# A hybrid decoder trunk: where the last head's row sums and its gate product stand in the program

## The chip, the cores and the metric

The kernel runs on one core of a Trainium2 chip. The metric is the device time of one execution in microseconds (us). Before and after are each run several times, and their medians are compared. Next to the runs stands one execution that the hardware profiler recorded; every row of a profile quoted here is from such an execution.

## The reference, cut to what matters

Two layers over 528 tokens (16 meta tokens and 512 of the sequence), model width 1024. Each layer normalises the residual stream, projects it with one large matrix, runs two token mixers side by side, gates their outputs, and adds the merged result back:

```python
h = rmsnorm(h_res, norm_gain[l])
proj = h @ w_in[l]          # u_pool z_pool c_q c_kv k_rope z_mla g_pool g_mla
y_pool = (pool_mix(u_pool, ...) * jax.nn.silu(z_pool)) @ pool_w_up[l]
o_mla = mla(c_q, c_kv, k_rope, pos, ...)            # 8 heads, causal softmax
y_mla = (o_mla * jax.nn.silu(z_mla)) @ mla_w_up[l]
merged = jax.nn.sigmoid(g_pool) * y_pool + jax.nn.sigmoid(g_mla) * y_mla
h_res = h_res + merged @ w_out[l]
```

For the change only the softmax of `mla` counts. A head's output is `exp(s - max) @ v`, divided by the row sum of the exponentials. The kernel leaves the division out of the head and multiplies the gate `silu(z_mla)` by the reciprocals of the row sums instead. The head's values, summed, are multiplied by that gate afterwards.

## The kernel before, in words

**Matrix products.** Every weight tile of 128x512 is fetched from DRAM into one of three buffers called `raw` (`wload`, L193; the fetch is L136, on SyncE's queue, SP), split by ScalarE (L206, `whi`) and VectorE (L207, `wlo`) into a high and a low part, and used by three matmuls for each product (`mm3`, L210: lines 211, 212, 213). A buffer `raw` comes free when L207 has read it; the third next fetch waits for that. Every second tile of `mu` in layer 1 (the second projection after attention, weights `wmu`) goes to a wider pair called `th`.

**The stream.** All products form one list in a fixed order (`register`): in each layer eight tiles `gm0` to `gm7` (the gate of attention, weights `win`), then eight `mu` (`wmu`), then eight `o` (`wout`). A `gm` result is taken out of its PSUM bank by VectorE in L1058; there are four such banks, `mm`. `stream` hands out this list in steps of six matmuls, and `step` (L271) adds each step's nominal time to a counter: 1280 ns with 512 columns (layer 1), 660 ns with 264 (layer 0). A `gm` tile is four steps in layer 1, eight in layer 0. `after(ns, fn)` (L281) registers a piece of other work that is written into the program at the first step at which the counter has gone on by `ns`; this is how attention is woven into the products. `newest[0]` is the last matmul written so far.

**The order on the engines.** The kernel is written in this order, and a planner (`schedule_with_timeline_sim=True`, L1303) then decides the order on each engine: it places an instruction when its inputs are ready by its own model, the one written first ahead of the others. An engine's queue is then fixed and works strictly in that order: on SP an instruction that waits holds all that are behind it. `behind(ins, other)` (L316) makes `ins` wait for `other`; `follow(ins, other)` (L312) sets only the order of two instructions of the same engine, without a wait.

**A head** (`head`, L825). The scores of one head are computed, exponentiated by ScalarE, which also gives the row sums `rs`, and turned in 32x32 blocks by VectorE (L856) into `attD`. The sum of the third part is added in L909, and L910 takes the reciprocals of all row sums. Then, for the head `h`:

- L916 writes the turned blocks to DRAM (`pdr<-attD`, 640 KB). For an odd head `meta_turn` also writes a small block (`mdr<-cq`, L959, written 2600 ns later) and reads it back much later (`racc<-mdr`, L955, three DMAs, 13000 ns later).
- `back` (L921), registered for 7800 ns later, for the last head 2600 ns later, reads the blocks back in an order that finishes the transpose: four DMAs `attE<-pdr` (L924), each behind `newest[0]`, and directly after them, by `follow`, the row sums leave for DRAM: `rdr<-rs`, L927, 2 KB, one piece of 16 bytes from each of 128 partitions.
- `sums` (L930), 2600 ns after `back`, reads the row sums back, spread over 64 partitions: `cq<-rdr`, L934, 128 KB. It needs the row sums to have landed in DRAM.
- `gate` (L936), for odd heads, is the product on GpSimd (L938): gate times reciprocals. For the last head it is registered 7800 ns after the head.
- `parts` (L962) splits the blocks read back (ScalarE L972 `th<-attE`, VectorE L973), and `pv` (L976) multiplies them with the values (TensorE L994 and L997, then L1002 and L1003 take the result out). `part2` (L1007), 6000 ns after the last head's `pv`, adds the meta tokens (TensorE L1009, which reads `racc`; VectorE L1012), multiplies by the gate (L1013) and splits the result for `mu`.

After head 7 the program goes on with gm tiles while head 6 and head 7 are finished (`go`, L1162).

Of the kernel before, what the change touches and what calls it, by code (L numbers as in the profile page):

```python
# [27 lines left out]
H = 8  # L28
# [27 lines left out]
LAG = 2000.0  # L56
TAIL = (9000.0, 9000.0)
SPL = 240
BACK = 7800.0
LATE = 13000.0  # L60
# [21 lines left out]
def trunk(ctx, tc, xT, xrow, mrow, pos, win, wkr, wqb, wkb, wvb, wgr, wpu, wmu, wout, gains, const, yT):  # L82
    nc = tc.nc
    pe, act, dve, gp, sp = nc.tensor, nc.scalar, nc.vector, nc.gpsimd, nc.sync
# [11 lines left out]
    def nm(s):  # L96
        uid[0] += 1
        return f"{s}_{uid[0]}"
# [7 lines left out]
    def att(tag):  # L106
        return sl.tile([P, NB * P], F32 if tag == "D" else F32R, tag=f"att{tag}", name=nm(f"att{tag}"), bufs=1 if tag == "D" else 2)
# [108 lines left out]
    newest = [None]  # L216
# [64 lines left out]
    def after(ns, fn):  # L281
        pend.append((clk[0] + ns, fn))
        pend.sort(key=lambda e: e[0])
# [28 lines left out]
    def follow(ins, other):  # L312
        tc.add_manual_dep(ins.ins, other.ins.name,
                          mybir.DependencyInfo(mybir.DependencyClass.NoSync, mybir.DependencyReason.SCHED_ONLY))

    def behind(ins, other):  # L316
        tc.add_manual_dep(ins.ins, other.ins.name,
                          mybir.DependencyInfo(mybir.DependencyClass.Sync, mybir.DependencyReason.DATA))
# [35 lines left out]
    class Layer:  # L354
# [470 lines left out]
        def head(self, h, kq, prev):  # L825
# [5 lines left out]
            rs = sm.tile([P, 5], F32, tag="rs", name=nm("rs"), bufs=2)  # L831
# [80 lines left out]
            row = rdr[self.l][h]  # L912
# [8 lines left out]
            def back():  # L921
                got.append(att("E"))
                for b in range(4):
                    read = sp.dma_start(got[0][32 * b:32 * b + 32, :].bitcast(F32).rearrange("k (a x) -> k a x", a=4),  # L924
                                        via[:, n * b:n * b + n].rearrange("(a k) x -> k a x", a=4))
                    behind(read, newest[0])
                follow(sp.dma_start(row.rearrange("a (p i) -> p (a i)", i=4), rs[:, 0:4]), read)  # L927
                after(BACK / 3, sums)

            def sums():  # L930
                if odd == 0:
# [4 lines left out]
            def gate():  # L936
                z, rb = self.zms[h // 2][:, NM:T].rearrange("p (i q) -> p i q", i=4), self.rb
                behind(gp.tensor_mul(z, z, rb[:, 0:512].rearrange("p (q i) -> p i q", i=4)), newest[0])  # L938

            after(BACK if h + 1 < H else BACK / 3, back)  # L940
            if odd == 1:
                after(LATE if h + 1 < H else BACK, gate)
            return h, got

        def meta_turn(self, pm):
# [362 lines left out]
```

## Time and profile before

| what | us |
|---|---|
| runs before | 755.31, 755.49, 753.53 |
| their median | 755.31 |
| the profiled execution, its own time | 755.48 |
| its span, first to last instruction | 753.7 |
| TensorE busy in the span | 748.1 |

The span is what the profile shows; 1.78 us of the profiled execution's own time lie around it (755.48 - 753.7). In rows of the timeline the first number is the start in us from the span's start, the second the duration; then come engine, line, operation, and the tiles as out<-in with the count of instructions merged into the row. In brackets stands how long the engine was idle before it, and what ended that. SPq is SP's queue: a row there is the issue of a DMA, not the transfer. In the chain of waits a row is start, duration, engine or DMA, and line or tiles; there the duration of a DMA is the time from its issue to its landing.

### The profile page before, as it was taken

What the parts mean: (1) busy time and instruction counts of PE and PEld (TensorE: products, weight loads), DVE (VectorE), ACT (ScalarE), POOL (GpSimd) and SP (SyncE); (2) the same over time, 40 slices, a digit from 0 to 9 for tenths busy, and PEclk for the clock granted to TensorE, in tenths of its full rate; (3) what the DMA queues carried; (4) which work ended last, traced back from release to release, by engine and by line L of the source; (5) the groups of instructions that cost most, each with busy time, mean ns of one, the idle gap of its engine ahead of it and who ended that gap; (6) DMA issues with size and microseconds to landing.
All of it is one profiled execution on the core that took longest, in us unless ns stands there. A gap on an engine that the chain in (4) does not pass through costs nothing.

```text
span 753.7 us, 14317 instructions
## 1 busy us (share of the span) xinstructions
PE 748.1 (99%) x5010; PEld 681.9 (90%) x5010; DVE 562.3 (75%) x1214; ACT 395.2 (52%) x864; POOL 241.8 (32%) x294
## 2 busy tenths in 40 slices
PE   9999999999999999999999999999999999999998
PEld 9999899999999999999997898887788888887887
DVE  5588777658999987694367478678589999966942
ACT  6755656554656555543254456455445665554321
POOL 2126404704552520161130264038043526102400
PEclk9999999999999999999999999999999999999999
DMA  8633223434766576425643332233356666763462
GB/s 280 179 103 118 70 81 91 112 96 142 206 163 177 170 202 176 129 91 165 183 135 91 108 113 73 82 91 107 105 151 216 181 175 189 203 167 98 129 223 87
DMA packets 72798, 106.55 MB, mean 141 GB/s; under 512 B 14051, under 2 KB 34915, under 8 KB 72726
## 3 DMA queue, kind: packets, MB, share of 16 engines
q1 hardware_dynamic: 72582, 105.38, 47.8%
q8 instruction: 39, 0.64, 0.4%
q14 instruction: 33, 0.27, 0.1%
q10 hardware_dynamic: 144, 0.26, 0.1%
HBM read 89.76 MB, written 15.85 MB: 140 GB/s over the span
## 4 chain that ended last, share of the span: by engine, by line
PE 94%; DMA 4%; SPq 1%; DVE 1%; ACT 0%; issue 0%; ACTq 0%; DVEq 0%
PE mm L211 28%; PE mm L213 28%; PE mm L212 28%; PE S L211 2%; PE S L213 2%; PE S L212 2%; DMA raw<-wmu 1%; PE o L994 1%; DMA rdr<-rs 1%; PE o L997 1%; PE S L891 1%; PE S L538 1%; PE S L504 0%; DMA raw<-win 0%; DMA cq<-rdr 0%; DMA xb<-xT 0%
## 5 line engine op out<-in xcount | busy, mean ns | idle before, releaser
L213 PE MATMUL mm<-hh,wlo 128*128 128x264 f32 (+2 forms) x1072 | 337.0, 316 | 0.0
L212 PE MATMUL mm<-hl,whi 128*128 128x264 f32 (+2 forms) x1072 | 336.4, 315 | 0.0
L211 PE MATMUL mm<-hh,whi 128*128 128x264 f32 (+2 forms) x1072 | 336.3, 315 | 0.0
L207 DVE TENSOR_TENSOR wlo<-raw,whi 128x512 fp32r<-128x512 f32 (+2 forms) x239 | 179.6, 754 | 87.5 <-ACT whi L206 83.9
L206 ACT ACTIVATE whi<-raw 128x512 fp32r<-128x512 f32 (+2 forms) x239 | 143.0, 600 | 167.3 <-PE mm L212 133.2
L211 PEld LDWEIGHTS mm<-hh,whi 128*128 128x128 f32 x1072 | 201.4, 188 | 14.1 <-DVE vt L704 0.8
L212 PEld LDWEIGHTS mm<-hl,whi 128*128 128x128 f32 x1072 | 201.6, 188 | 13.0
L213 PEld LDWEIGHTS mm<-hh,wlo 128*128 128x128 f32 x1072 | 200.9, 188 | 12.3
L652 POOL TENSOR_TENSOR racc<-racc,tmp 128x264 f32<-128x264 f32 (+1 forms) x15 | 14.9, 993 | 117.7 <-ACT tmp L651 117.7
L1069 POOL TENSOR_TENSOR tmp<-tmp,xb 128x264 f32<-128x264 f32 (+1 forms) x24 | 27.7, 1166 | 41.8 <-DVE tmp L1067 39.7
L821 POOL CAST qhl<-q 32x528 fp32r<-32x528 f32 (+1 forms) x32 | 27.6, 876 | 40.5 <-PE S L891 39.1
L843 DVE CUSTOM_DVE_ANT_0 S<-S,maskw,nqs 128x240 f32<-128x240 f32 (+4 forms) x80 | 37.9, 493 | 1.5 <-PE S L213 1.3
L211 PE MATMUL mm<-cq,whi 128*128 128x264 f32 (+1 forms) x108 | 34.7, 321 | 0.0
L212 PE MATMUL mm<-th,whi 128*128 128x264 f32 (+1 forms) x108 | 34.6, 321 | 0.0
L213 PE MATMUL mm<-u,wlo 128*128 128x264 f32 (+1 forms) x108 | 34.5, 320 | 0.0
L212 PE MATMUL mm<-cq,whi 128*128 128x264 f32 (+1 forms) x108 | 34.5, 321 | 0.0
L213 PE MATMUL mm<-cq,wlo 128*128 128x264 f32 (+1 forms) x108 | 34.5, 321 | 0.0
L211 PE MATMUL mm<-u,whi 128*128 128x264 f32 (+1 forms) x108 | 34.5, 319 | 0.0
L938 POOL TENSOR_TENSOR u<-u,cq 128x512 f32<-128x512 f32 x8 | 12.9, 1616 | 64.6 <-DMA cq<-rdr 41.2
L853 POOL COPY pm<-cq 128x16 f32<-128x16 f32 x32 | 17.9, 559 | 44.4 <-ACT cq L850 42.3
L850 ACT ACTIVATE cq<-S,bia 128x400 f32<-128x400 f32 (+2 forms) x48 | 24.4, 512 | 13.9 <-DVE bia L904 12.8
L973 DVE TENSOR_TENSOR attE<-attE,th 128x640 fp32r<-128x640 f32 x32 | 25.6, 828 | 6.1 <-ACT th L972 6.1
(305 smaller groups left out, 1401.2 us busy)
## 6 DMA issues: line engine op xcount, KB each, us to landing
raw<-win SPq DMA_DIRECT2D x143, 256.0 KB, 3.5
pdr<-attD SPq DMA_DIRECT2D x16, 640.0 KB, 3.6
attE<-pdr SPq DMA_DIRECT2D x64, 160.0 KB, 3.6
raw<-wout SPq DMA_DIRECT2D x32, 256.0 KB, 3.0
raw<-wpu SPq DMA_DIRECT2D x16, 256.0 KB, 2.7
raw<-wmu SPq DMA_DIRECT2D x16, 256.0 KB, 2.7
raw<-wqb SPq DMA_DIRECT2D x12, 256.0 KB, 2.6
xb<-xT SPq DMA_DIRECT2D x8, 264.0 KB, 5.6
```

What stands on the lines that cost most here:

```text
L206: act.activation(hi[:, :n], raw[:, :n], AF.Copy)
L207: dve.tensor_sub(lo[:, :n], raw[:, :n], hi[:, :n].bitcast(F32))
L211: first = pe.matmul(out, wh, xh, start=start, stop=False)
L212: pe.matmul(out, wh, xl, start=False, stop=False)
L213: newest[0] = pe.matmul(out, wl, xh, start=False, stop=stop)
L652: self.acc_last = gp.tensor_add(self.acc[:, a:b], self.acc[:, a:b], t[:, :b - a])
L821: gp.tensor_copy(d[r0:r0 + 32, x0:T], f[gq:gq + 32, x0:T])
L843: return dve.tensor_tensor_reduce(out=sv, in0=sv, in1=mask, scale=nqs[:, i, h:h + 1], scalar=3e38, op0=ALU.add, op1=ALU.min, accum_out=bia ...
L850: act.activation(pv, sv, AF.Exp, scale=-1.0, bias=bia[:, i:i + 1], accum_out=rs[:, c:c + 1])
L853: gp.tensor_copy(pm[:, i, 16 * odd:16 * odd + 16], pt[i][:, 0:NM])
L973: dve.tensor_sub(got[:, a:b], f[:, a:b], hi[:, a:b].bitcast(F32))
L1069: gp.tensor_add(t[:, :b - a], t[:, :b - a], self.am[m][:, a:b])
```

## The change

Only head 7 of each layer is touched (`h + 1 < H` is false). For the other heads the row leaves as before.

- The row sums of head 7 (the DMA of L927) are written into the program 2000 ns (`LAG`) of the step counter after `back`, where before they were written together with it. They no longer follow the last of the four reads; they are behind the newest matmul at that point.
- `sums` of head 7 comes 4600 ns after `back` where before it came 2600 ns after it; the distance between row and `sums` stays 2600.
- The gate product of the last head comes 9800 ns after the head where before it came 7800 ns after it.

No DMA, no product and no byte is added or removed.

```diff
-                follow(sp.dma_start(row.rearrange("a (p i) -> p (a i)", i=4), rs[:, 0:4]), read)
-                after(BACK / 3, sums)
+
+                def leave():
+                    follow(sp.dma_start(row.rearrange("a (p i) -> p (a i)", i=4), rs[:, 0:4]), read)
+                    after(BACK / 3, sums)
+
+                if h + 1 < H:
+                    leave()
+                else:
+                    after(LAG, lambda: behind(sp.dma_start(row.rearrange("a (p i) -> p (a i)", i=4), rs[:, 0:4]), newest[0]))
+                    after(LAG + BACK / 3, sums)
...
             if odd == 1:
-                after(LATE if h + 1 < H else BACK, gate)
+                after(LATE if h + 1 < H else BACK + LAG, gate)
```

## The prediction, made before the changed kernel was run

> **What bounds the kernel now.** I read the page first: the share of each engine, then who waited for whom, for TensorE and for SP's queue, then the chain of waits at the two places where head 7 ends.
>
> ```profile
> span 753.7 us, 14317 instructions
> PE 748.1 (99%) x5010; PEld 681.9 (90%) x5010; DVE 562.3 (75%) x1214; ACT 395.2 (52%) x864; POOL 241.8 (32%) x294
> ```
>
> TensorE is busy for 748.1 of 753.7 us. The whole list of what it waited for is three rows:
>
> ```profile
> PE mm L211 <- DVE cq L1058: 1.1, 1, 1.1
> PE wps L158 <- DVE na L774: 1.1, 1, 1.1
> PE S L994 <- ACT th L972: 0.2, 1, 0.2
> ```
>
> The second is the start of the kernel (the warming matmuls of L158), which the change doesn't reach. What any change of attention's order can win is therefore the first and the third row, about 1.3 us, which is under 0.2%. What it can lose has no such bound. The first row, on TensorE's timeline:
>
> ```profile
> 685.93 0.39 PE L212 MATMUL mm<-kn,th 128*128 128x512 f32 x1
> 686.16 0.40 PE L213 MATMUL mm<-q,th 128*128 128x512 f32 x1
> 687.70 0.47 PE L211 MATMUL mm<-q,whi 128*128 128x512 f32 x1 [1.14 <-DVE cq L1058]
> ```
>
> Matmuls of this shape start 0.23 us apart (685.93, 686.16); the next starts 1.54 us later. So the stall is 1.54 - 0.23 = 1.3 us, counted from start to start. The matmul is the first of `mu2` in layer 1 and waits for the bank that `gm7` leaves. The chain of waits says why that bank is late, and shows the same form in layer 0:
>
> ```profile
> 297.94 0.41 SPq L934
> 298.45 3.49 DMA raw<-win
> 302.58 1.36 ACT th L972 x2
> ...
> 669.51 4.02 DMA rdr<-rs
> 673.61 0.45 SPq L934
> 674.15 5.58 DMA raw<-wmu
> ...
> 680.41 0.79 DVE th L207
> 681.22 2.70 DMA raw<-wmu
> ...
> 684.69 0.68 DVE th L207
> 686.86 0.70 DVE cq L1058
> ```
>
> From the top of the lower part: head 7's row sums take 4.02 us to land. `sums` (L934) stands on SP until then, and a weight fetch behind it leaves only at 674.15. Its cast ends at 681.20, so the buffer `raw` comes free late, the next fetch leaves at 681.22, its cast (684.69) holds VectorE's queue, and the bank's L1058 comes last, at 686.86. In layer 0 it is shorter: a `win` fetch leaves behind L934 at 298.45, ScalarE's cast of it stands in front of L972, and L994 waits 0.2 us. Both stalls of TensorE begin at **SP waiting in L934 for the row sums of head 7**.
>
> **Where the row goes.** The title of the change says later. SP's queue in layer 1 and layer 0 says what "later" is measured against:
>
> ```profile
> 664.47 0.32 SPq L916 DMA_DIRECT2D pdr<-attD  x1
> 665.24 0.33 SPq L136 DMA_DIRECT2D raw<-win  x1
> 666.41 0.32 SPq L959 DMA_DIRECT2D mdr<-cq  x1
> 667.72 1.75 SPq L924 DMA_DIRECT2D attE<-pdr  x4
> 669.51 1.75 SPq L927 DMA_DIRECT2D rdr<-rs  x1
> 671.30 0.43 SPq L136 DMA_DIRECT2D raw<-win  x1
> 671.83 0.38 SPq L136 DMA_DIRECT2D raw<-wmu  x1
> ```
>
> ```profile
> 287.30 0.54 SPq L916 DMA_DIRECT2D pdr<-attD  x1
> 291.31 0.32 SPq L924 DMA_DIRECT2D attE<-pdr  x1
> 294.83 0.43 SPq L927 DMA_DIRECT2D rdr<-rs  x1
> 295.30 0.43 SPq L136 DMA_DIRECT2D raw<-win  x1
> 297.90 0.45 SPq L934 DMA_DIRECT2D cq<-rdr  x1
> ```
>
> The reads wait for the blocks to land in DRAM (issue 664.47, first read 667.72), and the row waits behind them because `follow` says so. Its own inputs are earlier. After the change it needs two things: the reciprocals, and the newest matmul one `LAG` after `back`. By the step counter `back` of layer 1 is written when `gm4` is half done and the row when `gm4` is complete; in layer 0 it is when the first of the two segments of `gm3` is complete. VectorE's rows give bounds for both (first layer 1, then layer 0, with the L1058 that takes this result out):
>
> ```profile
> 665.13 0.17 DVE L910 RECIPROCAL rs<-rs 128x4 f32<-128x4 f32 x1
> 666.38 0.69 DVE L1058 TENSOR_TENSOR cq<-mm,rinv 128x512 f32<-128x512 f32 x1
> 671.40 0.68 DVE L207 TENSOR_TENSOR wlo<-raw,whi 128x512 fp32r<-128x512 f32 x1
> ```
>
> ```profile
> 286.54 0.15 DVE L910 RECIPROCAL rs<-rs 128x4 f32<-128x4 f32 x1
> 290.65 0.41 DVE L1058 TENSOR_TENSOR cq<-mm,rinv 128x264 f32<-128x264 f32 x1
> ```
>
> Counting the L1058 of layer 1 back from 686.86 (`gm7`), 666.38 takes out `gm4`; the matmul is done by then. So the row can leave between 665.30 and 666.38, on a queue that is idle from 665.57 to 666.41 and from 666.73 to 667.72: **before the reads, about 3 to 4 us earlier than now**, not later. In layer 0 it can leave between 287.84, when SP is through with the blocks, and 290.65; the reads start at 291.31. The planner does pass instructions over others: the `wmu` fetch at 671.83 is written after `sums`, and leaves before it (673.61).
>
> **The change part by part.**
>
> - The row's DMA is neither added nor made larger, only moved past `mdr` and the four reads. Its issue (0.43 us in layer 0; 1.75 in layer 1) falls in the 2.15 us between 665.57 and 667.72, of which `mdr` takes 0.32. Both fit with 0.1 us left; a delay of the reads is bounded by 1.75 us and taken as 0, since 0.43 is the nearer row (a rival below prices the other end).
> - The added wait for the matmul: it holds SP, where `mdr`, the reads and the fetches are queued. Its end is at most 666.38, before `mdr` leaves now. Below it is 0, above it 666.38 - 665.57 = 0.8 us, still covered by the wait for the blocks until 667.72. Taken as 0.
> - `sums`, written two steps later than now: its matmul is in the first half of `gm5`, which is taken out at 670.80 at the latest (the next L1058 after 666.38 in VectorE's order); what decides is the row's landing:
>
> ```profile
> DMA to landing us min/median/max: 3.3/3.6/4.1
> 670.80 0.67 DVE L1058 TENSOR_TENSOR cq<-mm,rinv 128x512 f32<-128x512 f32 x1
> ```
>
> With the longest of the 16 rows, 665.6 + 4.1 = 669.7. The reads are issued by 669.47. So `sums` follows them almost without a wait, at about 669.7 (670.8 at worst), and the 1.75 us that the row takes now at 669.51 are free for it. The two fetches follow at about 670.2 and 670.7, where they leave at 671.30 and 671.83 now.
>
> - The next fetch, now at 674.15, then waits only for its buffer, which L207 frees at 671.40 + 0.68 = 672.08. It leaves at 672.1, **2.05 us earlier**. If the 1.3 us by which one issue is longer than the others (1.75 against 0.43) falls on another DMA of this stretch, it is still 672.4, 1.75 us earlier. With 5.58 us to landing, as now, the whole lower part of the chain moves forward by 1.75 to 2.05 us, more than the stall of 1.3. Gain: 1.3 us. What is late next is nothing in this stretch: after 687.70 no row of TensorE's waits follows.
> - In layer 0 the fetch at 298.45 waits for L934, which ends at 297.9; without it, it leaves behind the fetch at 295.30, some 2 us earlier. Gain: the 0.2 us of the third row.
> - The gate, 2000 ns later in the program: no DMA, one product on GpSimd, which waits for `sums`, and its reader L1013 comes after `pv` of head 7 and another 6000 ns of steps. Taken as 0; if it were late, GpSimd's next work would be late with it, which is that of `mu`.
>
> Sum: 755.48 - 1.3 - 0.2 = 753.98, so **754.0 us**, against a median of 755.31 that lies 0.17 us below the profiled execution. The forecast is a gain of 1.3 us, or 0.2%. The measurement tells about 0.3% (2.3 us) from no change, so this counts as the same.
>
> A rule that speaks against the change: the Trainium skill, page "DMA: Bandwidth & Descriptors", section "Queues, rings and completion order", has it that each DMA engine takes up the descriptors of a ring in the order of issue. By that rule the row, now ahead of the reads on the same queue, delays their data, which no row of this trace shows. The sum by it is the third rival's.
>
> **The rivals.**
>
> 1. *The wait is moved and not removed* (slower). If the planner puts the row where its words say, behind the reads and the two fetches, the row leaves at about 670.5 (669.47 and two issues of about 0.5). `sums` then holds SP until 670.5 + 4.02 = 674.5, the fetch leaves at 675.0 instead of 674.15, and the stall grows by 0.85: 756.3 us, layer 0's stall left as it is. The point from which it decides: the row's issue plus 4.02 has to be under 672.1 for the full gain, so it must leave before 668.1, ahead of the reads; at 669.51 nothing changes, and each us beyond costs one. With a landing of `racc` that is as much later, L1009 could add up to another us. For it: the words of the change; against it: the inputs are there 3 us before the reads.
> 2. *The transfer, not the queue, is the limit.* The fetch lands 5.58 us after its issue, the next one 2.70. If those 2.9 us are other transfers in its way, an earlier issue brings no earlier landing. Layer 1's stall stays, layer 0's goes: 755.3 us. For it: 5.58 against 2.70; against it: the reads and both earlier fetches would also be issued no later than now.
> 3. *The row delays the reads.* Then L972 of head 7, which waits for them, is late:
>
> ```profile
> 673.37 1.37 ACT L972 ACTIVATE th<-attE 128x640 fp32r<-128x640 f32 x2 [2.70 <-DMA attE<-pdr]
> 675.90 0.40 PE L994 MATMUL S<-th,vt 128*128 128x512 f32 x1
> ```
>
> L972 ends at 674.74, L994 starts at 675.90: 1.16 us of cover. The whole 1.75 us of delay cost 0.6 us: 754.6 us.
>
> 4. *The planner turns something else.* A new order on SP can put a cast on VectorE ahead of a bank's L1058 at another place, as 684.69 stands ahead of 686.86 now. One such stall of 1.3 us without the gains: 756.8 us; two, 758.1.
>
> **How the numbers follow.** The forecast has 0.55, the first rival 0.17, the second 0.12, the third 0.06, the fourth 0.10. The likeliest is 754.0. For the range, the runs before differ by 2 us among themselves (753.53 to 755.49), so I go down to 752.8 and up to 757.0, past the first and the first half of the fourth rival. Faster by over 0.3% (under 753.05) would need more than both stalls, so only the spread of runs: 0.06. Slower by over 0.3% (above 757.6) needs the first rival with a late `racc`, or two new stalls: 0.13. The rest, 0.81, is within 0.3%.
>
> **What would show it.** Right: on SP `rdr<-rs` of head 7 stands between the blocks' write and the first read in both layers; L934 follows the reads within half a us; the fourth next fetch leaves at about 672 and no longer right behind L934; TensorE's list of waits has only the start of the kernel. Wrong: `rdr<-rs` behind a read, L934 more than 2 us behind the DMA before it, or a row of waits for L1058, L972 or L1009 on TensorE. The prediction as a whole is wrong if a stall shows at a place that has nothing to do with head 7.

## The result, and the profile after

The changed kernel takes 755.78 us (median of 21 executions, 754.93 to 759.2), the kernel before, beside it on the same chip, 754.86 us (21 executions, 753.53 to 756.19). The ratio is 1.0017, with a 95% interval of 1.0010 to 1.0025; it is estimated from all executions of both, and isn't the quotient of the two medians (755.78 / 754.86 = 1.0012). The forecast was 754.0 us and a gain of 1.3 us. The time lies within 0.3% and inside the range, but the sign is the other one: a small, measurable loss. The profiled execution took 755.15 us with a span of 753.4, so 1.75 us lie around it, as before (1.78).

The page's first lines for the changed kernel, then the whole list of what TensorE waited for (us in total, times, longest us):

```profile
span 753.4 us, 14319 instructions
PE 748.4 (99%) x5010; PEld 682.3 (91%) x5010; DVE 562.2 (75%) x1214; ACT 395.7 (53%) x864; POOL 239.7 (32%) x294
```

```profile
PE wps L158 <- DVE na L774: 1.1, 1, 1.1
PE S L1002 <- ACT th L980: 0.4, 1, 0.4
PE S L1005 <- DVE attE L981: 0.3, 1, 0.3
```

Behind the changed place the lines stand 8 further down: the split L972 and L973 is now L980 and L981, the matmuls of `pv` L994 and L997 are L1002 and L1005, `sums` L934 is L942, the gate product L938 is L946. Head 7's row leaves in L935, `mdr` in L967, `racc` in L963.

Both stalls that the prediction wanted to remove are gone from the list (L211 behind the bank, and layer 0's). Two others stand in their place, both in `pv` of head 7 in layer 1. SP's queue at that place, to be held against the same stretch of before:

```profile
663.52 0.32 SPq L916 DMA_DIRECT2D pdr<-attD  x1
664.29 0.33 SPq L136 DMA_DIRECT2D raw<-win  x1
664.72 0.72 SPq L935 DMA_DIRECT2D rdr<-rs  x1
665.54 0.40 SPq L967 DMA_DIRECT2D mdr<-cq  x1
666.72 1.75 SPq L924 DMA_DIRECT2D attE<-pdr  x4
669.54 0.45 SPq L942 DMA_DIRECT2D cq<-rdr  x1
670.09 0.53 SPq L136 DMA_DIRECT2D raw<-win  x1
670.67 1.75 SPq L136 DMA_DIRECT2D raw<-wmu  x2
```

The row leaves ahead of `mdr` and the reads, and `sums` behind the reads and ahead of all three fetches. The reads are issued 3.20 us after the blocks (666.72 - 663.52), against 3.25 before (667.72 - 664.47). So their issue isn't late. Layer 0 shows the same order:

```profile
288.32 0.88 SPq L935 DMA_DIRECT2D rdr<-rs  x1
289.29 0.41 SPq L967 DMA_DIRECT2D mdr<-cq  x1
290.75 3.43 SPq L924 DMA_DIRECT2D attE<-pdr  x4
294.27 0.45 SPq L942 DMA_DIRECT2D cq<-rdr  x1
```

What is late is what the reads bring. ScalarE, VectorE and GpSimd of the changed kernel in layer 1, and then the rows of VectorE and GpSimd before:

```profile
674.90 1.37 ACT L980 ACTIVATE th<-attE 128x640 fp32r<-128x640 f32 x2 [4.75 <-DMA attE<-pdr]
675.67 2.04 DVE L981 TENSOR_TENSOR attE<-attE,th 128x640 fp32r<-128x640 f32 x1 [4.45 <-ACT th L980]
675.48 1.55 POOL L946 TENSOR_TENSOR u<-u,cq 128x512 f32<-128x512 f32 x1 [12.37 <-DMA cq<-rdr]
```

```profile
674.15 1.56 DVE L973 TENSOR_TENSOR attE<-attE,th 128x640 fp32r<-128x640 f32 x2 [2.07 <-ACT th L972]
679.08 1.55 POOL L938 TENSOR_TENSOR u<-u,cq 128x512 f32<-128x512 f32 x1 [15.02 <-DMA racc<-mdr]
```

Two things are to be seen. The cast L980 starts 674.90 - 666.72 = 8.18 us after the first read is issued; before it was 673.37 - 667.72 = 5.65. And the first half of VectorE's split takes 2.04 us, where both halves together took 1.56: the gate product on GpSimd, which the program now holds later, starts 3.6 us *earlier* than in this first profile of before (675.48 against 679.08), 0.19 us ahead of the split. (In a second profile of the kernel before, g1_before_again below, it starts at 676.82.) TensorE's timeline shows what the two cost:

```profile
675.50 0.40 PE L213 MATMUL mm<-hh,wlo 128*128 128x512 f32 x1
676.32 0.51 PE L1002 MATMUL S<-th,vt 128*128 128x512 f32 x1 [0.42 <-ACT th L980]
...
677.81 0.40 PE L213 MATMUL mm<-hh,wlo 128*128 128x512 f32 x1
678.50 0.45 PE L1005 MATMUL S<-attE,vt 128*64 128x512 f32 x1 [0.29 <-DVE attE L981]
```

From start to start the steps are 0.82 and 0.69 us, where 0.23 is usual: (0.82 - 0.23) + (0.69 - 0.23) = 0.59 + 0.46 = 1.05 us.

The chain of waits (start, duration, what) had the row sums' landing, SP in L934 and two fetches at this place before. Now it has one fetch, the split and `pv`:

```profile
671.25 6.35 DMA raw<-wmu
677.65 0.80 DVE attE L981
678.50 0.45 PE S L1005
```

The link from the fetch to the split is only inferred, from the fetch having landed last; L981 doesn't read `raw`. The rows of VectorE and GpSimd above say what held it.

### The profile page after: what moved, and what is told of

Same layout as the page of the kernel before. It is cut to its first block, busy times and chain, and to the rows that moved or that the text cites. A ratio compares the mean times of both kernels' runs of the same rounds, so it can differ in the third digit from the quotient of the medians.

```text
span 753.4 us, 14319 instructions
## 1 busy us (share of the span) xinstructions
PE 748.4 (99%) x5010; PEld 682.3 (91%) x5010; DVE 562.2 (75%) x1214; ACT 395.7 (53%) x864; POOL 239.7 (32%) x294
## 4 chain that ended last, share of the span: by engine, by line
PE 98%; DMA 1%; DVE 0%; ACT 0%; issue 0%; DVEq 0%
PE mm L213 29%; PE mm L211 29%; PE mm L212 29%; PE S L211 2%; PE S L213 2%; PE S L212 2%; PE o L1002 1%; PE o L1005 1%; DMA raw<-wmu 1%; PE S L891 1%; PE S L538 1%; PE wps L158 1%; PE S L504 0%; PE mm L1017 0%; PE S L1005 0%; PE mm L710 0%
## 5 line engine op out<-in xcount | busy, mean ns | idle before, releaser
L213 PE MATMUL mm<-hh,wlo 128*128 128x264 f32 (+2 forms) x1072 | 337.0, 316 | 0.0
L211 PE MATMUL mm<-hh,whi 128*128 128x264 f32 (+2 forms) x1072 | 336.2, 315 | 0.0
L207 DVE TENSOR_TENSOR wlo<-raw,whi 128x512 fp32r<-128x512 f32 (+2 forms) x239 | 181.5, 762 | 84.3 <-ACT whi L206 78.5
L211 PEld LDWEIGHTS mm<-hh,whi 128*128 128x128 f32 x1072 | 201.4, 188 | 14.0 <-DVE vt L704 0.8
L213 PEld LDWEIGHTS mm<-hh,wlo 128*128 128x128 f32 x1072 | 200.9, 188 | 12.3
L821 POOL CAST qhl<-q 32x528 fp32r<-32x528 f32 (+1 forms) x32 | 25.7, 818 | 39.5 <-PE S L891 38.2
L211 PE MATMUL mm<-cq,whi 128*128 128x264 f32 (+1 forms) x108 | 34.7, 321 | 0.0
L213 PE MATMUL mm<-u,wlo 128*128 128x264 f32 (+1 forms) x108 | 34.5, 320 | 0.0
L213 PE MATMUL mm<-cq,wlo 128*128 128x264 f32 (+1 forms) x108 | 34.5, 321 | 0.0
L211 PE MATMUL mm<-u,whi 128*128 128x264 f32 (+1 forms) x108 | 34.5, 319 | 0.0
L981 DVE TENSOR_TENSOR attE<-attE,th 128x640 fp32r<-128x640 f32 x32 | 27.2, 877 | 7.7 <-ACT th L980 7.7
L946 POOL TENSOR_TENSOR u<-u,cq 128x512 f32<-128x512 f32 x8 | 13.1, 1643 | 61.0 <-DMA cq<-rdr 56.6
```

What stands on the lines that cost most here:

```text
L207: dve.tensor_sub(lo[:, :n], raw[:, :n], hi[:, :n].bitcast(F32))
L211: first = pe.matmul(out, wh, xh, start=start, stop=False)
L213: newest[0] = pe.matmul(out, wl, xh, start=False, stop=stop)
L821: gp.tensor_copy(d[r0:r0 + 32, x0:T], f[gq:gq + 32, x0:T])
L981: dve.tensor_sub(got[:, a:b], f[:, a:b], hi[:, a:b].bitcast(F32))
```

## The experiments

The theory after the result, called theory A in the expectations: the row's DMA, 128 pieces of 16 bytes, ahead of the reads makes them land late, and `pv` of head 7 in layer 1 waits for the cast. Next to it stands a second claim: the stall of 1.3 us that was to be won is not in every execution. The rivals: the reads wait for their place in SP's queue, or for the read back of `sums`; the fetches behind the earlier read back of `sums` are what is late (theory B in the expectations); the loss is in layer 0 or elsewhere. All numbers of the table are from the profiled executions, in layer 1; "delay" is from the issue of the first read to the start of the cast. Times are medians, with the kernel before on the same chip beside them; the ratio is estimated as above. A kernel that ran once has its one time, which decides nothing on the time.

| kernel | ahead of the reads | delay us | time / before us | ratio, 95% interval |
|---|---|---|---|---|
| before (first profile) | nothing | 5.65 | | |
| g1_before_again | nothing | 6.33 | 753.79 / 755.00, one execution | |
| e1_layer0_only | nothing | 6.34 | 754.19 / 754.15 | 0.9999, 0.9990 to 1.0008 |
| e3_row_held | nothing | 6.23 | 754.17 / 754.15 | 1.0003, 0.9993 to 1.0012 |
| g3_row_behind_fetches | nothing | 6.20 | 754.34 / 755.00 | 0.9994, 0.9986 to 1.0003 |
| after | the row, 128 x 16 B | 8.18 | 755.78 / 754.86 | 1.0017, 1.0010 to 1.0025 |
| e2_layer1_only | the row | 8.74 | 755.82 / 754.15 | 1.0018, 1.0005 to 1.0032 |
| e4_double_row | the row, twice | 7.68 | 755.82 / 754.15 | 1.0019, 1.0011 to 1.0028 |
| f3_row_on_act | the row, ScalarE's queue | 7.56 | 755.39 / 753.92 | 1.0018, 1.0009 to 1.0027 |
| g2_gate_late | the row | 8.99 | 755.43 / 755.00 | 1.0007, 0.9997 to 1.0016 |
| f1_small_ahead | 128 x 16 B, nobody reads | 8.02 | 754.86 / 753.92 | 1.0016, 1.0007 to 1.0026 |
| g4_few_ahead | 16 x 16 B | 7.43 | 755.60 / 755.00, one execution | |
| j2_pieces_32 | 128 x 32 B | 5.67 | 754.31 / 754.33, one execution | |
| h3_pieces_64 | 128 x 64 B | 6.37 | 753.30 / 754.11, one execution | |
| h4_pieces_256 | 128 x 256 B | 6.40 | 754.36 / 754.11, one execution | |
| f2_wide_ahead | 128 x 512 B | 6.51 | 754.37 / 753.92 | 1.0006, 0.9998 to 1.0015 |

The delay is a measure of the landing. The trace keeps 16 landing marks of each read; half of those of the last read are in 4.7 to 5.0 us after the first read's issue where nothing stands ahead, and 6.0 to 6.5 us after it in the six kernels with 128 or more pieces of 16 bytes. In f1_small_ahead and f3_row_on_act the last mark (674.86 and 675.18) stands 0.1 us in front of the cast (674.96 and 675.29); the bracket of these two rows names a matmul that ended at the same time.

**Which layer: e1_layer0_only and e2_layer1_only.** The first has the change in layer 0 alone (the condition gets `or self.l != 0`), the second in layer 1 alone:

```diff
-                if h + 1 < H:
+                if h + 1 < H or self.l != 1:
...
-                after(LATE if h + 1 < H else BACK + LAG, gate)
+                after(LATE if h + 1 < H else BACK + LAG * (self.l == 1), gate)
```

> The change made in layer 0 alone; layer 1 as before. Theory A (the row ahead of the reads makes head 7's blocks land late, and the product with the values waits): in layer 0 the reads land late too (5.7 us instead of 3.0 to 3.3) but the product is far enough behind, so TensorE shows no wait there; the 0.2 us of the kernel before go, layer 1 keeps its own. 0 to 0.3 us faster than before, ratio 0.9995 to 1.0. Theory B (the fetches behind the earlier read of the row sums are what is late): the fetches of gm6 and gm7 in layer 0 land late, a wait of TensorE on a cast there, about 0.5 us slower, ratio 1.0005 to 1.001.

> The change made in layer 1 alone; layer 0 as before. Theory A: all of the loss is here. TensorE waits in L1002 and L1005 of head 7 for L980 and L981, 0.7 us or more together, L980 stands idle over 4 us for the reads; ratio that of the whole change, 1.001 to 1.0025. Theory B: no more than half of the loss, ratio 1.0 to 1.001, with a wait on a cast (L206, L207).

Layer 0 alone changes nothing, layer 1 alone gives the loss of the whole change. TensorE's waits of e2_layer1_only at head 7, and the reads and their cast in e1_layer0_only:

```profile
PE S L1002 <- ACT th L980: 1.0, 1, 1.0
PE S L1005 <- DVE attE L981: 0.3, 1, 0.3
```

```profile
666.57 1.74 SPq L924 DMA_DIRECT2D attE<-pdr  x4
672.91 1.37 ACT L980 ACTIVATE th<-attE 128x640 fp32r<-128x640 f32 x2 [3.12 <-DMA attE<-pdr]
```

In e1_layer0_only layer 1 has the order of before, and the wait at L211 that the first profile showed there is not in its list (which has 0.3 us at another L211, 5 us after the start of the kernel). Its span is 751.8 us. In its layer 0 the row is ahead of the reads too, but nothing waits for them there: by the landing marks the last read is in at 297.27, and ScalarE starts its cast only at 299.84, behind a cast of weights.

**The row kept behind the reads: e3_row_held.** The row is written at the later point of the change and also follows the last read, which gives SP the order of before.

```diff
+                    def leave_late():
+                        ins = sp.dma_start(row.rearrange("a (p i) -> p (a i)", i=4), rs[:, 0:4])
+                        follow(ins, read)
+                        behind(ins, newest[0])
...
+                    after(LAG, leave_late)
```

> The change with one line more: the row is written as late as in the change, and is also kept behind the last read. The row sums, their read and the gate product have the change's places in the program, but on SP the row cannot pass the reads. Theory A: the loss is gone, as is the gain: ratio 1.0 within 0.0008, TensorE's waits are those of before (L1058's bank, up to 1.3 us). Theory B or a cost of the later gate product: the loss stays, ratio 1.001 or more.

The loss is gone, and there is no gain either. The expectation missed in one point: the wait of before, at L211 for the bank, isn't there. TensorE waits for nothing but the start of the kernel:

```profile
PE wps L158 <- DVE na L774: 1.1, 1, 1.1
```

**The kernel before once more: g1_before_again.** No edit.

> The kernel before once more, for a second profile of it. If its stall of 1.3 us before mu2 stands in every execution: TensorE waits about 1.1 us for L1058 again, span 753.5 or more. If it depends on how the transfers fall in one execution: no such wait, span 751.8 to 752.3, as in the two variants whose layer 1 has the order of before.

Its list of TensorE's waits has only the start of the kernel, and its span is 752.0 us, not 753.7. SP's queue, with ScalarE's cast of the reads, shows where it parts from the first profile:

```profile
667.41 1.74 SPq L924 DMA_DIRECT2D attE<-pdr  x4
669.20 0.43 SPq L927 DMA_DIRECT2D rdr<-rs  x1
669.67 0.44 SPq L136 DMA_DIRECT2D raw<-win  x1
...
673.74 1.37 ACT L972 ACTIVATE th<-attE 128x640 fp32r<-128x640 f32 x2 [3.35 <-DMA attE<-pdr]
673.88 0.45 SPq L934 DMA_DIRECT2D cq<-rdr  x1
674.43 0.54 SPq L136 DMA_DIRECT2D raw<-wmu  x1
```

`sums` still waits until 673.88 (673.61 in the first profile), and the fetch behind it leaves at 674.43, even later than 674.15. Yet no stall follows. Two things differ. The row's issue is shorter, 0.43 us against 1.75, and with it the fetch of `win` leaves earlier, 669.67 against 671.30. And the fetch behind `sums` lands sooner: its cast starts 3.7 us behind its issue (678.17 - 674.43), where the first profile shows 5.58 us to landing. The first alone doesn't make the stall: j2_pieces_32 (below) has a row issue of 1.72 us there, its fetch behind `sums` leaves at 674.20, and it has no stall either. Its cast starts 4.4 us behind that issue:

```profile
678.63 0.63 ACT L206 ACTIVATE th<-raw 128x512 fp32r<-128x512 f32 x1 [1.70 <-DMA raw<-wmu]
```

So the order of the queue alone doesn't make the 1.3 us; they came with the late landing of that fetch in one execution. Why it landed late there stays open.

**The row alone, with nothing that depends on it: f1_small_ahead and f2_wide_ahead.** To the kernel before, an extra write to DRAM is added ahead of `mdr` and the reads of layer 1; nobody reads it. In f1 it has the row's shape, 128 pieces of 16 bytes; in f2 it has 128 pieces of 512 bytes, 32 times the bytes.

```diff
+                if self.last and h + 1 == H:
+                    behind(sp.dma_start(spare_row.rearrange("a (p i) -> p (a i)", i=4), cst[:, 0:4]), made)
```

> The kernel before, with one DMA more in layer 1: 128 pieces of 16 bytes of the constants go to a DRAM tensor that nobody reads, at the place on SP where the change puts the row (before mdr and the reads of head 7). Row, sums and gate product stay. If it is the small pieces ahead of the reads that make them late: over 4 us idle in front of L972 of head 7, TensorE waits 0.4 to 1.4 us in L994, ratio 1.001 to 1.003. If the earlier read of the row sums (L934 ahead of the fetches) makes the loss: no wait in L994, ratio 0.9995 to 1.0005.

> The same with 128 pieces of 512 bytes (64 KB) in place of 16 bytes. If any DMA to DRAM ahead holds the reads, or its bytes count: reads as late as with the small pieces or later, ratio 1.001 to 1.003. If only the small pieces do it: the reads are late by no more than the 64 KB take, 0.2 to 0.5 us, within the cover of 1.2 us, no wait in L994, ratio 0.9995 to 1.0005.

SP, ScalarE and the wait of TensorE in f1_small_ahead, then SP and ScalarE in f2_wide_ahead (the split is L976 in both):

```profile
664.90 0.73 SPq L926 DMA_DIRECT2D sprow<-cst  x1
666.94 1.75 SPq L928 DMA_DIRECT2D attE<-pdr  x4
675.09 0.45 SPq L938 DMA_DIRECT2D cq<-rdr  x1
674.96 1.36 ACT L976 ACTIVATE th<-attE 128x640 fp32r<-128x640 f32 x2 [4.93 <-PE mm L212]
```

```profile
PE S L998 <- ACT th L976: 0.6, 1, 0.6
```

```profile
667.78 1.74 SPq L928 DMA_DIRECT2D attE<-pdr  x4
674.29 1.37 ACT L976 ACTIVATE th<-attE 128x640 fp32r<-128x640 f32 x2 [3.54 <-DMA attE<-pdr]
```

The 2 KB write makes the cast 1.7 us later than in g1_before_again (8.02 against 6.33) and brings the wait and the loss. With the 64 KB write it is 0.2 us later, which is within the 0.7 us by which the kernels with nothing ahead differ, and `pv` doesn't wait. f2's time tells less than its trace: its interval reaches from no change to most of the loss. In f1 the read back of `sums` leaves only at 675.09, after the cast has begun: it cannot be what holds the reads. So the first rival (place in the queue) and the second (`sums`) are out; the bytes are not it either.

**How many pieces: e4_double_row and g4_few_ahead.** e4 is the changed kernel with the row written twice, the second time to spare DRAM; g4 is f1 with 16 pieces.

```diff
+                        behind(sp.dma_start(spare_row[self.l].rearrange("a (p i) -> p (a i)", i=4), rs[:, 0:4]), newest[0])
```

```diff
-                    behind(sp.dma_start(spare_row.rearrange("a (p i) -> p (a i)", i=4), cst[:, 0:4]), made)
+                    behind(sp.dma_start(spare_row[:, 0:64].rearrange("a (p i) -> p (a i)", i=4), cst[0:16, 0:4]), made)
```

> The change, with the row of head 7 written twice, the second time to a DRAM tensor that nobody reads (one DMA of 2 KB more in each layer). Theory A with the row's pieces of 16 bytes as what holds the reads: reads land later still by 0.5 to 2 us, the wait in L1002 grows by as much, ratio against before 1.002 to 1.004. If only the issue of one more DMA counts: its 0.4 us lie in SP's idle time before the reads, ratio as the change, 1.001 to 1.0025.

> The variant with the extra small DMA ahead of the reads in layer 1, with 16 pieces of 16 bytes in place of 128, one for each DMA engine. If each piece costs its part (8 for each engine make 1.5 us): the reads are late by 0.2 us, their first packets come as without it, no wait in L994. If one small piece holds an engine as long as eight: reads late by 1.5 us, the median of their packets 3.8 to 4.1 us behind the first issue instead of 2.4, a wait of 0.4 us or more.

Twice the pieces didn't add: 7.68 us of delay against 8.18, ratio 1.0019 against 1.0017 (TensorE's wait was longer, 1.4 us, but e2_layer1_only, with one row, has 1.0). So the expected growth didn't come. An eighth of the pieces still gave 7.43 us and 0.9 us of wait, in one execution. By the other sign that the expectation for g4 named it came out the first way: half of the last read's landing marks are in after 5.1 us, as with nothing or wide pieces ahead (4.7 to 5.2), against 6.5 in f1; only the last mark is late (7.33 us, against 5.6 to 6.2 with nothing ahead). So the delay of the cast is not in proportion to the pieces, but with 16 of them most of the data come as without; that the price doesn't depend on the count is not shown.

**Which queue: f3_row_on_act.** The row is issued from ScalarE's DMA queue.

```diff
-                    after(LAG, lambda: behind(sp.dma_start(row.rearrange("a (p i) -> p (a i)", i=4), rs[:, 0:4]), newest[0]))
+                    after(LAG, lambda: behind(act.dma_start(row.rearrange("a (p i) -> p (a i)", i=4), rs[:, 0:4]), newest[0]))
```

> The change, with head 7's row issued from ScalarE's DMA queue instead of SP's, in both layers. If what counts is the place ahead of the reads on the same queue: the reads land as before (L980 idle for about 3 us), no wait in L1002, and the row still lands early, ratio 0.9985 to 1.0003. If the pieces hold the 16 DMA engines whatever queue they come from: reads late again, ratio 1.001 to 1.0025.

```profile
665.38 0.33 ACTq L935 DMA_DIRECT2D rdr<-rs  x1
667.73 1.74 SPq L924 DMA_DIRECT2D attE<-pdr  x4
675.29 1.36 ACT L980 ACTIVATE th<-attE 128x640 fp32r<-128x640 f32 x2 [4.64 <-PE mm L213]
```

The delay is 7.56 us and the loss remains (1.0018, 1.0009 to 1.0027). The order within one queue's ring, which the prediction took from the Trainium skill as the ground of its third rival, is therefore not needed for it. The Trainium skill, page "DMA: Bandwidth & Descriptors", section "Issuing engines are not separate DMA queues", says that DMAs of all issuing engines run on the same 16 engines and interleave there; this run agrees.

**Which size: j2_pieces_32, h3_pieces_64, h4_pieces_256.** f2 with narrower pieces; the edit is only the width (8, 16 or 64 numbers).

```diff
-                    behind(sp.dma_start(spare, cst[:, 0:128]), made)
+                    behind(sp.dma_start(spare[:, 0:8], cst[:, 0:8]), made)
```

> The kernel before with an extra write of 128 pieces of 32 bytes ahead of the reads of layer 1. Pieces of 16 bytes gave 8.0 us from the first read to the cast, pieces of 64 bytes 6.4. If a limit in size lies at or below 32 bytes: 6.2 to 6.5 us. If it lies above 32: 7.5 to 8.7. In between if the cost falls off evenly from 16 to 64 bytes.

> The kernel before with an extra write of 128 pieces of 64 bytes ahead of the reads of layer 1. If the count of pieces under some size holds the reads, whatever the bytes, the cast of the reads starts 7.5 to 8.7 us after the first read is issued, as with pieces of 16 bytes. If the cost falls off evenly between 16 and 512 bytes, about 7.5 us. If only pieces of 16 bytes do it, 6.2 to 6.5 us.

> The same with 128 pieces of 256 bytes. Under a limit in size that lies at 512 bytes: 7.5 to 8.7 us from the first read to the cast, as with 16 bytes. With a cost that falls off evenly: about 7 us. With a limit below 256 bytes: 6.2 to 6.5 us.

SP and ScalarE of j2_pieces_32, then of h3_pieces_64:

```profile
667.59 1.75 SPq L928 DMA_DIRECT2D attE<-pdr  x4
673.26 1.37 ACT L976 ACTIVATE th<-attE 128x640 fp32r<-128x640 f32 x2 [2.71 <-DMA attE<-pdr]
```

```profile
666.08 1.75 SPq L928 DMA_DIRECT2D attE<-pdr  x4
672.45 1.37 ACT L976 ACTIVATE th<-attE 128x640 fp32r<-128x640 f32 x2 [2.91 <-DMA attE<-pdr]
```

None of the three holds the reads (5.67, 6.37 and 6.40 us, one execution each); the wait of 0.7 us in h4's list is in layer 0. j2 lies below all that was forecast for it, like the first profile of before (5.65), with which it shares the long issue behind the reads. There is no even fall from 16 to 512 bytes: pieces of 16 bytes did it, pieces of 32 didn't. One thing was not kept apart: the pieces of 16 bytes stand next to each other in DRAM, the wider ones lie 512 bytes apart. Whether it is the size or the neighbourhood was not tried.

**The gate product: g2_gate_late.** The changed kernel, in layer 1 with the gate product 8000 ns further on; SP's order stays.

```diff
-                after(LATE if h + 1 < H else BACK + LAG, gate)
+                after(LATE if h + 1 < H else BACK + LAG + 8000 * self.last, gate)
```

> The change, with the gate product of head 7 in layer 1 written 8000 ns later; the order on every engine is that of the change. If the gate product on GpSimd, running beside L981 on VectorE, makes that one long (2.77 us for two instead of 1.56) and so the wait in L1005: L981 takes 1.56 us again, the wait in L1005 (0.3) goes, the wait in L1002 stays; ratio 0.0002 to 0.0005 under that of the change, 1.0005 to 1.002. If the two have nothing to do with each other: L981 2.77 us and the wait as in the change.

```profile
676.84 1.56 DVE L981 TENSOR_TENSOR attE<-attE,th 128x640 fp32r<-128x640 f32 x2 [5.38 <-DMA racc<-mdr]
678.78 1.83 POOL L946 TENSOR_TENSOR u<-u,cq 128x512 f32<-128x512 f32 x1 [15.33 <-PE mm L213]
```

```profile
PE S L1002 <- ACT th L980: 1.5, 1, 1.5
```

The split is back at 1.56 us and the wait at L1005 is gone, while the late cast stays (8.99 us, and 1.5 us of wait). The ratio is 1.0007, 0.9997 to 1.0016; the interval doesn't tell it from no change, and overlaps that of the change. What shows the stretch is the trace, not the time.

**More cover for the late cast: f4_pv_held, h1_cover_more, h2_pv_held_again, j1_held_and_gate_late.** The changed kernel with `pv` of head 7 in layer 1 later: nine matmuls (f4, and again as h2), three matmuls (h1), nine matmuls and the late gate of g2 (j1).

```diff
-            hosts, last = list(hosts), [None]
+            hosts, last = list(hosts), [newest[0] if self.last and h + 1 == H else None]
...
-            fill_now(2600)
+            fill_now(7680 if self.last else 2600)
```

```diff
-            fill_now(2600)
+            fill_now(5200 if self.last else 2600)
```

> The change, with the product of head 7 with its values in layer 1 placed 9 matmuls (2.1 us) later among those of gm7; VectorE and ScalarE take the cast for mu2 before that for mu3. If the loss is only that product's wait for late blocks (up to 1.6 us): it goes, TensorE waits for nothing but the start, ratio 0.9985 to 1.0003. If late fetches or anything else made the loss: ratio stays 1.001 or more, with a wait elsewhere.

> The change, with head 7's pv in layer 1 three matmuls of gm later (0.69 us at 0.23 us each); the orders of ScalarE, VectorE, GpSimd and SP are those of the change. Theory (the reads land late behind the small pieces, and the loss is TensorE's wait for the cast of them): the wait at L1002 falls from 0.4-1.5 to 0-0.8 us, the time lies halfway between the change and the kernel before, ratio 1.0005 to 1.0012. Rival (the loss is something other than that wait, spread over the stage): ratio 1.0015 to 1.0020, as for the change itself.

> The kernel of f4_pv_held once more, nine matmuls of cover (2.1 us). If the wait at L1002 is the whole loss, the executions lie at the kernel before, 0.9995 to 1.0005, with no second group 3 us above. If the order of casts that comes with it costs time of its own, the second group of some 3 us more shows again, and the profile, if it falls on one, has a wait at L211 for VectorE or ScalarE.

> The change with both waits met at once in layer 1: nine matmuls of cover ahead of head 7's pv, and the gate product 8000 ns later, so that it no longer starts ahead of VectorE's half of the split. The row stays ahead of the reads. Theory (the loss is the late cast and the stretched split, nothing else): L981 takes 1.56 us, no wait at L1002 or L1005, ratio 0.9995 to 1.0006. Rival (the stage loses something besides these two waits): ratio 1.0009 or more, as for h2_pv_held_again or the change itself.

| kernel | time / before us | ratio, 95% interval | wait at L1002 | wait at L1005 |
|---|---|---|---|---|
| f4_pv_held | 755.03 / 753.92 | 1.0022, 1.0010 to 1.0034 | none | none |
| h1_cover_more | 755.49 / 754.11 | 1.0022, 1.0013 to 1.0031 | none | 0.8 |
| h2_pv_held_again | 754.75 / 754.11 | 1.0009, 1.0000 to 1.0019 | none | 1.0 |
| j1_held_and_gate_late | 755.61 / 754.33 | 1.0013, 1.0002 to 1.0024 | none | 0.8 |

f4's profiled execution (754.18) is one of its faster ones; that it shows no wait doesn't explain the median of 755.03. Three matmuls of cover took the wait from L1002 and put it at L1005, with the time as before: my expectation for h1 missed, since it reckoned with the late cast alone, and the stretched split is the later of the two. Nine matmuls took some of the loss at most. In j1 the gate product, though later in the program, started 0.1 us ahead of the second half of the split, and that half was stretched to 2.18 us:

```profile
677.03 2.92 DVE L981 TENSOR_TENSOR attE<-attE,th 128x640 fp32r<-128x640 f32 x2 [4.28 <-ACT th L980]
```

```profile
677.67 1.59 POOL L946 TENSOR_TENSOR u<-u,cq 128x512 f32<-128x512 f32 x1 [12.94 <-PE mm L213]
```

So j1 didn't make the state that it was made for (its list also has 0.5 us at L213, in layer 0), and it decides nothing on whether the two waits are the whole loss. f4 had four of its twelve executions at 757.1 to 757.9 us; the same kernel as h2 had none above 755.9 in eleven. These four stay unexplained.

**The words of the change taken literally: g3_row_behind_fetches.** The kernel before with the row of layer 1 really later: behind the reads and two fetches, `sums` behind the third fetch and `racc`, the gate 7500 ns later.

```diff
-                follow(sp.dma_start(row.rearrange("a (p i) -> p (a i)", i=4), rs[:, 0:4]), read)
-                after(BACK / 3, sums)
+                def leave():
+                    ins = sp.dma_start(row.rearrange("a (p i) -> p (a i)", i=4), rs[:, 0:4])
+                    follow(ins, read)
+                    if last:
+                        behind(ins, newest[0])
+                    after(BACK / 3, sums)
...
+                if last:
+                    after(7500, leave)
```

> The kernel before, with head 7's row of layer 1 put where the words of the change put it: behind the reads and also behind the two next weight fetches; its read (L942 or near) comes behind the third fetch and racc. If small pieces hold what comes behind them in the DMA engines: the reads land as before, no wait in L994; the third fetch and racc are the ones held, by about 1.5 us, which the cover may or may not take: ratio 0.9985 to 1.001, at most the stall before mu2 of 1 us. If the row's place makes no difference as long as the reads are ahead of it: ratio 0.9995 to 1.0005.

With nothing ahead of the reads (6.20 us of delay) the time is 0.9994 of before, 0.9986 to 1.0003: not to be told from it. No kernel of this study is clearly faster than the kernel before.

## Why the prediction was wrong, step by step

- **Where the row goes: right.** It stands between the blocks and the first read in both layers, 1.20 us after the issue of the blocks in layer 1 (664.72 - 663.52; the bounds were 0.83 to 1.91). `sums` follows the reads, and all three fetches come behind it. The added wait for the matmul costs nothing, since the reads are issued no later.
- **`sums` without a wait: nearly right.** It starts 1.07 us behind the reads' last issue (669.54 against 666.72 + 1.75), not within half a us: the row took up to 4.82 us from its issue (669.54 - 664.72), more than the 4.1 that was reckoned. The fetch that left at 674.15 now leaves at 671.25, and the old stall is gone; but it takes 6.35 us to land, not the 5.58 that the sum took over.
- **The gain of 1.3 us: mis-sized, in most of the profiled executions there was nothing to win.** The step took a stall from one profiled execution for a property of the queue's order. In g1_before_again, e1_layer0_only and e3_row_held, which have the same order there, `pv` and `mu2` in layer 1 wait for nothing. The sign of it stood in the numbers given: the profiled execution (755.48) was among the slower ones shown, 1.95 us above the fastest (753.53), which is more than the whole stall. In layer 0 the mechanism was right: the cast in front of L994 starts at 300.54 in the changed kernel and at 299.84 in e1_layer0_only, against 302.58 before, and the wait is gone in both. But that wait is 0.2 us in the first profile, 0.7 in h4_pieces_256 and none in g1_before_again, which have the same order there, and it is too small for e1's time to show it (0.9999, 0.9990 to 1.0008).
- **The step that failed: "a delay of the reads is bounded by 1.75 us and taken as 0".** The row is not free ahead of the reads. In the six kernels of the table that have 128 or more pieces of 16 bytes ahead, the cast comes 7.56 to 8.99 us after the first read; where nothing stands ahead, 5.65 to 6.34. (With more cover, in f4, h1, h2 and j1, it is 7.85 to 8.44.) The price is 1.2 to 3.3 us of delay, 1.85 for the changed kernel against g1_before_again (8.18 - 6.33): not 0, and not bounded by 1.75. The bound was wrong because it took the issue's duration for the whole price; the delay arises in the transfers, where no issue shows it. Where the reads come in time, the cast ends 0.1 to 1.3 us ahead of `pv` (1.16 in the first profile), so that the delay outlasts this cover, and TensorE waits 0.4 to 1.5 us. This is the third rival, with its place right, its chance (0.06) too small and its ground (one queue's ring) not needed, as f3_row_on_act shows.
- **"The gate ... Taken as 0": wrong too.** Later in the program is not later in time: the product waits for `sums`, which the change brings forward. Counted from the first read, the product starts at 8.76 us, against 9.41 in g1_before_again, and the split at 8.95 against 7.10. So they meet mostly because the late reads push the split 1.85 us back, and for the smaller part because the product comes earlier. Price: 1.2 us on the split's first half (2.04 us, where both halves together take 1.56), 0.3 us of wait at L1005 in the changed kernel.
- **Rivals 1, 2 and 4.** The wait was not moved behind the fetches (1), and no other place shows a new stall (4). Of the second there is a piece of truth: the stall came with one fetch that landed late (5.58 us, against 3.7 in g1_before_again), and the fetch that the change issues earlier took longer still, 6.35 us.

What stays open: why pieces of 16 bytes hold transfers behind them for 1 to 2 us and pieces of 32 don't, and whether their being next to each other in DRAM has a part in it; whether the two waits are the whole loss (the two stalls are 1.05 us of the 1.6 us by which the span exceeds that of e1_layer0_only, 753.4 against 751.8; j1 was to settle it and didn't); and f4's four executions.

## What to carry to other kernels

A stall of 1 us in one profile of a kernel that is bound elsewhere is first to be found in a second execution before it is counted as a gain; the spread of the times shown already says whether it can be in all of them. A DMA moved past others is to be priced by what it does to their landing, and not by its issue, small pieces above all. And an instruction written later runs earlier if what it waits for comes earlier: look at what it will then run beside.

## What the runs showed of the hardware that was not expected

- **Small pieces.** A write of 128 pieces of 16 bytes to DRAM, 2 KB, issued 2.0 us ahead of four reads of 160 KB each made the cast of their data 1.7 us late (f1_small_ahead, 8.02 us against 6.33); issued from ScalarE's queue, the row did so by 1.2 us (f3_row_on_act, 7.56). 16 such pieces made the cast 1.1 us late (7.43), by the last of the data alone; 128 pieces of 32 bytes did not (5.67), nor did 64 KB in pieces of 512 (6.51). The Trainium skill, page "DMA: Bandwidth & Descriptors", section "Specifications", puts the size under which a transfer is read, modified and written back at 512 bytes. These runs show no effect on the reads behind from 32 bytes up, and one at 16; that a read-modify-write is what holds the reads was not shown.
- **GpSimd beside VectorE.** In the changed kernel the gate product runs from 675.48 to 677.03; the half of the split that starts at 675.67 ends at 677.71, 0.68 us behind it. In j1_held_and_gate_late the product ends at 679.26 and the split at 679.95, 0.69 us behind it. Undisturbed, two halves take 1.56 us together. So the split looks to stand still until the product is done. The Trainium skill, page "SBUF — State Buffer", section "Who interferes with whom", has it that a VectorE instruction with two inputs in SBUF contends with a GpSimd instruction that reads SBUF, that the ports they share are an exclusive lock, and that the order of issue decides who blocks; the trace agrees, with the product 0.19 us ahead and the split as the one that is held.
